# Low parts of the output-projection weights on GpSimd, and attention tiles of layer 0 opened in another order

## The chip, the core and the metric

The kernel is one program on one core of a Trainium2 chip (trn2). The metric is the device time of one execution in microseconds (us); lower is better. TensorE is called PE here, VectorE DVE, ScalarE ACT, GpSimd POOL, and SyncE's DMA queue SP, as the profile does.

## What is computed

A two-layer diffusion backbone over 512 latent tokens and 256 context tokens of width 1024. Each layer is a mixer and then an MLP, and each of the two ends in a residual sum and a layer norm:

```python
x = layer_norm(ALPHA * x + m_lat[2] * y_lat, ln_g[l, 0], ln_b[l, 0])
x = layer_norm(ALPHA * x + m_lat[5] * mlp(x * (1 + m_lat[4]) + m_lat[3], mlp_w1[l], mlp_w2[l]), ln_g[l, 1], ln_b[l, 1])
```

Here `y_lat` is the mixer's heads times `w_out`, and `mlp(u)` is `square(relu(u @ w1)) @ w2`. In layer 0 the same is done for the context tokens. The mixer of layer 0 runs gated linear attention (GLA) beside banded-window attention (GQA); the mixer of layer 1 runs RWKV-7 beside latent attention. All is in float32.

## The kernel before

Every dense product is made from three passes: each float32 operand is split into a high part (`whi`, `hi`, rounded to the fp32r format by ACT, L323) and a low part (`wlo`, `lo`, the remainder, a subtraction on DVE, L324), and `mm3` (L341 to L348) issues high by high (L344), high by low activation (L346) and low weight by high (L348). `weights` (L326) opens the tiles of one weight block of 128x1024 (`wraw` from the DMA, 5 buffers in layer 0's second half and shared with the `araw` loads; `whi` and `wlo`, 2 buffers each) and calls `split` (L321), whose last argument can name another engine for the low part.

`project` (L1001) makes an output projection in two parts of the tokens: in layer 0 all 512 latent tokens (part 0) and then the 256 context tokens (part 1). In each part it goes over eight weight blocks d = 0 to 7; in layer 0 the blocks are loaded and split again for part 1, in layer 1 they are kept (`keep`, `kept`). After part 0, the layer norm of the latent tokens (`norm`, L1038) is a generator that is advanced twice after each block of part 1. So beside the matmuls of part 1 these run:

- L1054 and L1062: mean and variance on PE, from `sums` and the squares (L1066, ACT); L1074 is the reciprocal root `lnr`.
- L1078: DVE multiplies `z` by `lnr`, eight pieces (here z0 to z7).
- L1092: DVE makes `lnu`, L1091: ACT makes the high part of the next activations, L1094: POOL makes their low part `actlo`, again eight pieces each (lnu0 to lnu7, lo0 to lo7).
- L1020 and L1024: DVE adds each block's product into `z` and `sums`.

Behind the projection come the first two weight blocks of the next dense stage, called m0 and m1 below (L323, L324 again). Layer 0 has two such projections: the mixer's (the **first site**, 475 to 517 us of the trace) and the MLP's last (the **second site**, 1042 to 1084 us).

`mixer0` (L858) starts the attention at about 200 us: it closes the weight pool, opens the pool `mb` in its space, and opens there some constants (`zerob`, `identb`, `maskb`, L973 to L981), then the level tiles of GLA (`gla_setup`, L486, with memsets of POOL, L494 and L496), then in `gqa` (L712) the tiles `mE`, `sel` (three small ACT operations, L728), `q2` and `gp`. A tile `mt`, from which `maskb` is cast, takes one of the four `Dt` buffers that GLA's decays also use (L597).

The order in which each engine runs its instructions is made at build time by a scheduler from priorities and dependencies. Every engine runs its own list strictly in order.

## Time and profile before

| what | value |
|---|---|
| median of 3 runs | 2068.6 us (2066.54 to 2073.67) |
| profiled execution | 2074.32 us |
| its span, first to last instruction | 2072.4 us |
| PE busy | 1942.7 us, 94% |
| DVE busy | 1315.2 us, 63% |
| ACT busy | 962.1 us, 46% |
| POOL busy | 297.2 us, 14% |
| mean granted clock of PE | 0.968 |

Busy shares are averages over the whole program. A row of the timeline gives the start of an instruction (or of several alike), how long it took, its engine, line and tiles, and in brackets how long its engine stood idle before it and what it waited for.

### The profile page before, as it was taken

How to read it: one execution, taken by the hardware profiler on the slowest of the kernel's cores; microseconds unless marked ns; L12 is line 12 of the kernel's file. 1: busy time of each engine (PE TensorE's matmuls, PEld its weight loads, DVE VectorE, ACT ScalarE, POOL GpSimd, SP SyncE). 2: the span in 40 equal slices, each digit the busy share in tenths (PEclk: the TensorE clock that was granted, in tenths of full speed). 3: DMA queues.
4: the chain of work that ended last, by engine and by line, in shares of the span. 5: the costliest groups of instructions: out<-in, count | busy, mean ns of one | idle time of the engine just before them, and what ended most of it. 6: DMA issues, size and time to landing. Idle time of an engine off the chain costs nothing.

```text
span 2072.4 us, 35378 instructions
## 1 busy us (share of the span) xinstructions
PE 1942.7 (94%) x14256; PEld 1617.3 (78%) x14256; DVE 1315.2 (63%) x2394; ACT 962.1 (46%) x1852; POOL 297.2 (14%) x503
## 2 busy tenths in 40 slices
PE   7998799999999999999989999988889889999998
PEld 6887666677788888888877877757776788888887
DVE  8785999638897566534484554467876655544454
ACT  5526777535522222222255655766664544333332
POOL 0002666302100000000021020023231020000001
PEclk9999799999999999999999998998999999999999
DMA  8650000063454455313243100000000503332241
GB/s 297 203 171 14 1 2 1 1 211 104 140 169 138 143 158 152 112 51 97 82 147 120 46 9 13 13 9 2 3 7 29 173 28 96 110 94 86 92 137 41
DMA packets 67048, 181.67 MB, mean 88 GB/s; under 512 B 7491, under 2 KB 12355, under 8 KB 66757
## 3 DMA queue, kind: packets, MB, share of 16 engines
q1 hardware_dynamic: 66884, 179.42, 27.8%
q8 instruction: 112, 1.84, 0.4%
q14 instruction: 52, 0.42, 0.1%
HBM read 172.83 MB, written 5.51 MB: 86 GB/s over the span
## 4 chain that ended last, share of the span: by engine, by line
PE 71%; DVE 15%; ACT 7%; issue 3%; DMA 2%; POOL 1%; SPq 0%; DVEq 0%; ACTq 0%; POOLq 0%
PE mm L346 18%; PE mm L348 18%; PE mm L344 17%; DMA araw<-in_ada_r_dram 2%; PE var L1062 2%; PE ms L1454 2%; PE mo L1480 1%; PE gab L1612 1%; DVE wlo L324 1%; DVE aprod L392 1%; DVE z L1078 1%; PE go L789 1%; DMA wraw<-in_w_m_dram 1%; PE gx L1728 1%; PE st L1494 1%
## 5 line engine op out<-in xcount | busy, mean ns | idle before, releaser
L323 ACT CAST whi<-wraw 128x1024 fp32r<-128x1024 f32 (+2 forms) x253 | 221.5, 879 | 639.7 <-PE mm L346 559.9
L344 PE MATMUL mm<-acthi,whi 128*128 128x512 f32 (+1 forms) x1464 | 444.8, 350 | 15.4 <-ACT whi L323 13.5
L348 PE MATMUL mm<-acthi,wlo 128*128 128x512 f32 (+1 forms) x1464 | 439.1, 346 | 8.7 <-DVE wlo L324 8.5
L346 PE MATMUL mm<-actlo,whi 128*128 128x512 f32 (+1 forms) x1464 | 443.8, 349 | 2.4 <-POOL actlo L1094 2.2
L324 DVE TENSOR_TENSOR wlo<-wraw,whi 128x1024 fp32r<-128x1024 f32 (+2 forms) x253 | 256.5, 1017 | 219.0 <-ACT whi L323 214.6
L344 PEld LDWEIGHTS mm<-acthi,whi 128*128 128x128 f32 x1464 | 251.1, 191 | 55.6 <-ACT whi L323 16.0
L348 PEld LDWEIGHTS mm<-acthi,wlo 128*128 128x128 f32 x1464 | 251.8, 192 | 48.8 <-DVE wlo L324 12.6
L346 PEld LDWEIGHTS mm<-actlo,whi 128*128 128x128 f32 x1464 | 251.2, 191 | 39.0 <-POOL actlo L1094 4.1
L348 PE MATMUL mm<-hh,wlo 128*128 128x512 f32 (+1 forms) x832 | 253.1, 342 | 3.6 <-DVE wlo L324 3.6
L346 PE MATMUL mm<-hl,whi 128*128 128x512 f32 (+1 forms) x832 | 254.7, 344 | 0.1
L344 PE MATMUL mm<-hh,whi 128*128 128x512 f32 (+1 forms) x832 | 254.1, 343 | 0.0
L1094 POOL TENSOR_TENSOR actlo<-lnu,acthi 128x256 fp32r<-128x256 f32 (+1 forms) x48 | 60.8, 1281 | 720.6 <-DVE lnu L1092 632.9
L348 PEld LDWEIGHTS mm<-hh,wlo 128*128 128x128 f32 x832 | 144.3, 189 | 24.3 <-DVE wlo L324 4.2
L346 PEld LDWEIGHTS mm<-hl,whi 128*128 128x128 f32 x832 | 143.6, 189 | 19.3 <-issue 0.7
L344 PEld LDWEIGHTS mm<-hh,whi 128*128 128x128 f32 x832 | 142.8, 189 | 20.0 <-issue 1.0
L1166 DVE SCALAR_TENSOR_TENSOR z<-mm,mod,z 128x512 f32<-128x512 f32 (+1 forms) x144 | 94.1, 659 | 97.4 <-PE mm L348 97.4
L392 DVE SCALAR_TENSOR_TENSOR araw<-araw,scb 128x1024 f32<-128x1024 f32 x80 | 97.8, 1222 | 53.4 <-DMA araw<-in_ada_r_dram 52.5
L1020 DVE SCALAR_TENSOR_TENSOR z<-mm,mod,z 128x256 f32<-128x256 f32 (+1 forms) x64 | 34.9, 548 | 82.0 <-PE mm L348 80.9
L323 ACT CAST hh<-relu 128x512 fp32r<-128x512 f32 (+1 forms) x100 | 50.5, 534 | 76.3 <-DVE relu L1118 76.3
L616 POOL TENSOR_TENSOR lk<-kd,Dt 64x128 f32<-64x128 f32 x144 | 76.2, 529 | 31.9 <-ACT Dt L598 12.3
L392 DVE SCALAR_TENSOR_TENSOR aprod<-araw,scb 128x1024 bf16<-128x1024 f32 x48 | 58.6, 1221 | 26.8 <-DMA araw<-in_ada_r_dram 26.7
L324 DVE TENSOR_TENSOR hl<-relu,hh 128x512 fp32r<-128x512 f32 (+1 forms) x100 | 56.1, 587 | 26.5 <-ACT hh L323 26.1
(461 smaller groups left out, 3241.4 us busy)
## 6 DMA issues: line engine op xcount, KB each, us to landing
araw<-in_ada_r_dram SPq DMA_DIRECT2D x80, 512.0 KB, 3.7
wraw<-in_w_dram SPq DMA_DIRECT2D x72, 512.0 KB, 3.6
wraw<-in_w_dram SPq DMA_DIRECT2D x144, 256.0 KB, 2.7
wraw<-in_w_s_dram SPq DMA_DIRECT2D x31, 512.0 KB, 3.7
wraw<-in_w_o_dram SPq DMA_DIRECT2D x22, 512.0 KB, 3.7
scraw<-in_ada_sc_dram SPq DMA_DIRECT2D x8, 512.0 KB, 5.7
shraw<-in_ada_sh_dram SPq DMA_DIRECT2D x8, 512.0 KB, 6.0
x<-in_xT_dram SPq DMA_DIRECT2D x8, 384.0 KB, 5.7
```

Source lines behind the costliest of these rows:

```text
L323: self.nc.scalar.copy(hi, raw)
L324: (eng or self.nc.vector).tensor_tensor(lo, raw, hi.bitcast(F32), op=ALU.subtract)
L344: mm(o, whi, ahi[:, sl], start=first, stop=False)
L346: mm(o, whi, alo[:, sl], start=False, stop=False)
L348: mm(o, wlo, ahi[:, sl], start=False, stop=last)
L392: self.nc.vector.scalar_tensor_tensor(pr, raw, 1.0, self.scb[:, w], op0=ALU.mult, op1=ALU.mult, accum_out=out(w))
L616: nc.gpsimd.tensor_tensor(K[r, :, x], kk[r, :, x], d[r, :, x], op=ALU.mult)
L1020: nc.vector.scalar_tensor_tensor(zs, o, self.mod[:, l, self.wh(i, parts), g, d:d + 1], zs, op0=ALU.mult, op1=ALU.add)
L1062: nc.tensor.matmul(var, self.c('o1024', 0, P), sq, start=(k == 0), stop=(k == KT - 1))
L1094: eng.tensor_tensor(lo[:, k, sl], u, hi[:, k, sl].bitcast(F32), op=ALU.subtract)
L1166: nc.vector.scalar_tensor_tensor(z[:, d, sl], o, self.mod[:, l, self.wh(i, parts), 5, d:d + 1], z[:, d, sl], op0=ALU.mult, op1=ALU.add)
L1454: mm(s_[:, j], a[:, c], b[:, j * 384:j * 384 + 384], start=st, stop=sp_)
```

## The change

It does three things.

1. `weights` takes an engine for the low part, and `project` gives it POOL for the blocks d = 1, 3, 5 and 7 of every part after the first. In layer 0 that moves 4 of the 8 low parts of part 1 from DVE to POOL at each site, 8 instructions of 128x1024 in all. In layer 1 the blocks of the second half are the kept ones, and nothing moves.
2. In the attention of layer 0, `gla_setup` is called before the constants, so the level tiles and their memsets come first and `zerob`, `identb` and `maskb` after them; one `q2` and one `gp` buffer are opened in the middle of the level tiles (`late`, called at level 8) and handed to `gqa` through `early`.
3. `sel` lives in the outer pool `m0` (`mx_`), whose space was not used by weights.

```diff
--- before.py
+++ after.py
@@ -323,7 +323,7 @@
         self.nc.scalar.copy(hi, raw)
         (eng or self.nc.vector).tensor_tensor(lo, raw, hi.bitcast(F32), op=ALU.subtract)
 
-    def weights(self, src, n=1024, keep=None, lead=PW):
+    def weights(self, src, n=1024, keep=None, lead=PW, eng=None):
 
         raw = self.wp.tile([P, 1024], F32, tag="wraw", name="wraw")
         pool, bufs, d = (self.wp, 2, '') if keep is None else (keep[0], 1, keep[1])
@@ -334,7 +334,7 @@
             m = n // len(src)
             for i, s in enumerate(src):
                 self.nc.sync.dma_start(raw[:, i * m:i * m + m], s)
-            self.split(raw[:, :n], hi[:, :n], lo[:, :n])
+            self.split(raw[:, :n], hi[:, :n], lo[:, :n], eng)
         return hi[:, :n], lo[:, :n]
 
     def mm3(self, whi, wlo, ahi, alo, first, last, outs):
@@ -483,7 +483,7 @@
         nc.scalar.activation(tmp, tmp, AF.Ln, bias=self.c('one'))
         nc.scalar.activation(out, tmp, AF.Exp, scale=-1.0)
 
-    def gla_setup(self, m0):
+    def gla_setup(self, m0, mid=lambda: None):
 
         nc = self.nc
         i = len(self.lev)
@@ -494,6 +494,8 @@
             nc.gpsimd.memset(lk[h], 0.0)
             if h >= 16:
                 nc.gpsimd.memset(lq[h], 0.0)
+            if h == 8:
+                mid()
         self.lev.append((lk, lq))
 
     def gla_head(self, m0, mx_, h, qd, kd, vt, a1T, g):
@@ -709,7 +711,7 @@
             for _ in a:
                 yield
 
-    def gqa(self, m0, mx_, queries, KS, K2, vg, hi, lo):
+    def gqa(self, m0, mx_, queries, KS, K2, vg, hi, lo, early):
 
 
 
@@ -723,7 +725,7 @@
             nc.gpsimd.memset(t, 0.0)
             mE.append(t)
         sink = slice(96, 99)
-        sel = m0.tile([99, 192], F32R, name="sel")
+        sel = mx_.tile([99, 192], F32R, name="sel")
         for i in range(3):
             nc.scalar.activation(sel[sink, i * 64:i * 64 + 64], self.c('ident', 0, 64)[sink], AF.Identity,
                                  scale=0.0, bias=self.c('one')[sink] if i != 1 else 0.0)
@@ -732,7 +734,7 @@
 
         def scores(h):
             kv, qs = h // 4, QS[h]
-            q2[h] = Q2 = m0.tile([99, T], F32R, name="q2", bufs=2)
+            q2[h] = Q2 = early.pop('q2') if 'q2' in early else m0.tile([99, T], F32R, name="q2", bufs=2)
 
             nc.gpsimd.memset(Q2[64:67].bitcast(F32), 0.0)
             for t0, n in PARTS:
@@ -800,7 +802,8 @@
                             mm(b[:, (n - n0) * P:(n - n0 + 1) * P], self.identb, self.maskb[0 if n < j else 1],
                                start=False, stop=False)
                 mm(b, K2[kv][:, ks], Q2[0:67, qr], start=False, stop=True)
-                p = m0.tile([P, 512], F32, name="gp", bufs=3)[:, 0:(n1 - n0) * P]
+                p = early.pop('gp') if 'gp' in early else m0.tile([P, 512], F32, name="gp", bufs=3)
+                p = p[:, 0:(n1 - n0) * P]
                 nc.scalar.activation(p, b, AF.Exp)
                 pv()
                 pend.append((ob[:, qr], j, p, j == 4))
@@ -970,6 +973,12 @@
             mhi, mlo = self.act_tiles()
             self.psum(PG[0], u=PG[1], q=PG[2], qo=PG[3])
             with tc.tile_pool(name="mb", bufs=1, reuse_waits="tile") as mb:
+                early = {}
+
+                def late():
+                    early['q2'] = mb.tile([99, T], F32R, name="q2", bufs=2)
+                    early['gp'] = mb.tile([P, 512], F32, name="gp", bufs=3)
+                self.gla_setup(mb, late)
                 self.zerob = mb.tile([P, P], BF16, name="zerob")
                 nc.gpsimd.memset(self.zerob, 0.0)
                 self.identb = mb.tile([P, P], BF16, name="identb")
@@ -979,7 +988,6 @@
                 nc.sync.dma_start(mt, self.a['band'])
                 for i in range(2):
                     nc.gpsimd.tensor_copy(self.maskb[i], mt[:, i * P:(i + 1) * P])
-                self.gla_setup(mb)
 
                 def queries(i):
 
@@ -989,7 +997,7 @@
                             nc.scalar.copy(a[r, sl], qg[i][r, sl])
                             nc.vector.tensor_tensor(a[o, sl], qg[i][r, sl], a[r, sl].bitcast(F32), op=ALU.subtract)
                     return mhi.k(4 + i), mlo.k(4 + i)
-                att = self.gqa(mb, m0, queries, KS, K2, vg, mhi, mlo)
+                att = self.gqa(mb, m0, queries, KS, K2, vg, mhi, mlo, early)
                 for i, _ in enumerate(self.gla(mb, setup, g, qd, kd, og, mhi, mlo)):
                     if i % 5 < 2:
                         next(att, None)
@@ -1009,7 +1017,8 @@
         for i, (t0, m) in enumerate(parts):
             sl = slice(t0, t0 + m)
             for d in range(KT):
-                wh, wl = kept.get(d) or self.weights(ws[d], keep=keep and (keep, d), lead=lead)
+                wh, wl = kept.get(d) or self.weights(ws[d], keep=keep and (keep, d), lead=lead,
+                                                      eng=nc.gpsimd if i and d % 2 else None)
                 if keep:
                     kept[d] = wh, wl
                 o = self.bank("mm")[:, :m]
```

Three places of the instruction order matter. The numbers in the names are those of the tiles.

DVE at the first site, after the second `lnu`, before. `wlo_5042`, `wlo_5079`, `wlo_5116` are the low parts of blocks 5, 6 and 7 of part 1; `mm_4993` is the product of block 4.

```order
L324 TENSOR_TENSOR wlo_5042<-wraw_5040,whi_5041 128x1024
L1092 TENSOR_SCALAR lnu_4978<-z_4504,gb_4824 128x512
L1078 TENSOR_TENSOR z_4504<-z_4504,lnr_4931 128x512
L324 TENSOR_TENSOR wlo_5079<-wraw_5077,whi_5078 128x1024
L1092 TENSOR_SCALAR lnu_4983<-z_4504,gb_4824 128x512
L1020 SCALAR_TENSOR_TENSOR z_4504<-mm_4993,mod_117,z_4504 128x256
L1078 TENSOR_TENSOR z_4504<-z_4504,lnr_4931 128x512
L1024 TENSOR_TENSOR sums_4524<-sums_4524,z_4504 128x256
L1092 TENSOR_SCALAR lnu_5021<-z_4504,gb_4824 128x512
L324 TENSOR_TENSOR wlo_5116<-wraw_5114,whi_5115 128x1024
```

The same stretch of DVE with the change:

```order
L1087 TENSOR_TENSOR z_4504<-z_4504,lnr_4931 128x512 x2
L1101 TENSOR_SCALAR lnu_4978<-z_4504,gb_4824 128x512
L1101 TENSOR_SCALAR lnu_4983<-z_4504,gb_4824 128x512
L1029 SCALAR_TENSOR_TENSOR z_4504<-mm_4993,mod_117,z_4504 128x256
L1087 TENSOR_TENSOR z_4504<-z_4504,lnr_4931 128x512
L324 TENSOR_TENSOR wlo_5079<-wraw_5077,whi_5078 128x1024
L1033 TENSOR_TENSOR sums_4524<-sums_4524,z_4504 128x256
L1101 TENSOR_SCALAR lnu_5021<-z_4504,gb_4824 128x512
L1087 TENSOR_TENSOR z_4504<-z_4504,lnr_4931 128x512 x2
L1101 TENSOR_SCALAR lnu_5026<-z_4504,gb_4824 128x512
```

Blocks 5 and 7 have left this queue, and block 6 (`wlo_5079`) now stands behind one more `z` and one more `lnu`. The low parts of m0 and m1 (`wlo_5157`, `wlo_5163`) stand further down: that of m0 was ahead of the last `z` and the last two `lnu`, and is now behind all of them.

POOL at the first site with the change. Before, the eight `actlo` stood there alone.

```order
L324 TENSOR_TENSOR wlo_4841<-wraw_4839,whi_4840 128x1024
L324 TENSOR_TENSOR wlo_4936<-wraw_4934,whi_4935 128x1024
L1103 TENSOR_TENSOR actlo0_4790<-lnu_4968,acthi0_4788 128x512
L1103 TENSOR_TENSOR actlo0_4790<-lnu_4973,acthi0_4788 128x512
L324 TENSOR_TENSOR wlo_5042<-wraw_5040,whi_5041 128x1024
L1103 TENSOR_TENSOR actlo0_4790<-lnu_4978,acthi0_4788 128x512
L1103 TENSOR_TENSOR actlo0_4790<-lnu_4983,acthi0_4788 128x512
L1103 TENSOR_TENSOR actlo0_4790<-lnu_5021,acthi0_4788 128x512
L324 TENSOR_TENSOR wlo_5116<-wraw_5114,whi_5115 128x1024
L1103 TENSOR_TENSOR actlo0_4790<-lnu_5026,acthi0_4788 128x512
L1103 TENSOR_TENSOR actlo0_4790<-lnu_5031,acthi0_4788 128x512
L1103 TENSOR_TENSOR actlo0_4790<-lnu_5036,acthi0_4788 128x512
```

POOL makes blocks 1 and 3 ahead of the first `actlo`, block 5 behind the second and block 7 behind the fifth. The second site has the same lists with other tile numbers.

DVE at the start of the attention, before:

```order
L990 TENSOR_TENSOR actlo0_1897<-qg0_82,actlo0_1897 64x512
L597 TENSOR_TENSOR Dt_2041<-ld_1576 128x256
L618 TENSOR_TENSOR lq64_1_1917<-qd0_91,Dt_1952 64x2x64 x2
L618 TENSOR_TENSOR lq32_1_1921<-qd0_91,Dt_1997 64x4x32 x2
L964 SCALAR_TENSOR_TENSOR og_90<-mm_1777,col_65,og_90 128x512
L964 SCALAR_TENSOR_TENSOR og_90<-mm_1778,col_65,og_90 128x256
L597 TENSOR_TENSOR Dt_2060<-ld_1576 128x256
L990 TENSOR_TENSOR acthi0_1895<-qg0_82,acthi0_1895 64x512
L990 TENSOR_TENSOR acthi1_1896<-qg0_82,acthi1_1896 64x256
L990 TENSOR_TENSOR actlo1_1898<-qg0_82,actlo1_1898 64x256
L990 TENSOR_TENSOR acthi0_1895<-qg1_83,acthi0_1895 64x512
```

and with the change:

```order
L998 TENSOR_TENSOR actlo0_1897<-qg0_82,actlo0_1897 64x512
L620 TENSOR_TENSOR lq64_1_1907<-qd0_91,Dt_1954 64x2x64 x2
L620 TENSOR_TENSOR lq32_1_1911<-qd0_91,Dt_1998 64x4x32 x2
L967 SCALAR_TENSOR_TENSOR og_90<-mm_1777,col_65,og_90 128x512
L967 SCALAR_TENSOR_TENSOR og_90<-mm_1778,col_65,og_90 128x256
L998 TENSOR_TENSOR acthi0_1895<-qg0_82,acthi0_1895 64x512
L998 TENSOR_TENSOR acthi1_1896<-qg0_82,acthi1_1896 64x256
L998 TENSOR_TENSOR actlo1_1898<-qg0_82,actlo1_1898 64x256
L998 TENSOR_TENSOR acthi0_1895<-qg1_83,acthi0_1895 64x512
L998 TENSOR_TENSOR acthi1_1896<-qg1_83,acthi1_1896 64x256
L998 TENSOR_TENSOR actlo0_1897<-qg1_83,actlo0_1897 64x512
```

The decays `Dt_2041` and `Dt_2060` no longer stand ahead of the splits of the queries (L990, now L998); they come after ten of those splits and behind the first row maximum (L749, now L751). The second row maximum stood ahead of GLA's `ld` (L514) and its scans (L524), and now stands behind four of the scans.

## Rows read from the trace of the kernel before

**Rows 1.** Timeline of DVE, first site: start us, us, instruction, idle before.

```profile
473.62 1.22 DVE L324 TENSOR_TENSOR wlo<-wraw,whi 128x1024 fp32r<-128x1024 f32 x1
...
490.02 1.29 DVE L1078 TENSOR_TENSOR z<-z,lnr 128x512 f32<-128x512 f32 x2 [2.63 <-ACT lnr L1074]
491.23 0.54 DVE L1092 TENSOR_SCALAR lnu<-z,gb 128x512 f32<-128x512 f32 x1
491.69 0.48 DVE L1020 SCALAR_TENSOR_TENSOR z<-mm,mod,z 128x256 f32<-128x256 f32 x1
492.08 1.45 DVE L1092 TENSOR_SCALAR lnu<-z,gb 128x512 f32<-128x512 f32 x1
493.46 0.41 DVE L1024 TENSOR_TENSOR sums<-sums,z 128x256 f32<-128x256 f32 x1
493.79 1.76 DVE L1078 TENSOR_TENSOR z<-z,lnr 128x512 f32<-128x512 f32 x1
495.48 1.21 DVE L324 TENSOR_TENSOR wlo<-wraw,whi 128x1024 fp32r<-128x1024 f32 x1
...
497.67 2.30 DVE L324 TENSOR_TENSOR wlo<-wraw,whi 128x1024 fp32r<-128x1024 f32 x1
```

**Rows 2.** Timeline of POOL, first site.

```profile
491.95 1.31 POOL L1094 TENSOR_TENSOR actlo<-lnu,acthi 128x512 fp32r<-128x512 f32 x1 [73.69 <-DVE lnu L1092]
493.68 1.33 POOL L1094 TENSOR_TENSOR actlo<-lnu,acthi 128x512 fp32r<-128x512 f32 x1 [0.42 <-DVE lnu L1092]
497.29 1.59 POOL L1094 TENSOR_TENSOR actlo<-lnu,acthi 128x512 fp32r<-128x512 f32 x1 [2.29 <-DVE lnu L1092]
```

**Rows 3.** Timeline of PE, first site: first use of block 1, then the waits.

```profile
475.99 0.28 PE L348 MATMUL mm<-acthi,wlo 128*128 128x256 f32 x1
...
496.75 0.58 PE L348 MATMUL mm<-acthi,wlo 128*128 128x256 f32 x1 [2.16 <-DVE wlo L324]
...
504.40 0.39 PE L348 MATMUL mm<-acthi,wlo 128*128 128x256 f32 x1 [0.21 <-DVE wlo L324]
...
508.30 0.50 PE L348 MATMUL mm<-acthi,wlo 128*128 128x512 f32 x1 [0.53 <-DVE wlo L324]
...
512.91 0.50 PE L348 MATMUL mm<-acthi,wlo 128*128 128x512 f32 x1 [1.55 <-DVE wlo L324]
...
516.93 0.70 PE L1054 MATMUL mu<-sums,col 128*128 128x256 f32 x2 [0.56 <-DVE sums L1024]
```

**Rows 4.** Timeline of PE, second site: waits from m0 on.

```profile
1075.84 0.50 PE L348 MATMUL mm<-acthi,wlo 128*128 128x512 f32 x1 [0.53 <-DVE wlo L324]
...
1081.58 0.50 PE L346 MATMUL mm<-actlo,whi 128*128 128x512 f32 x1 [0.92 <-POOL actlo L1094]
...
1083.44 0.98 PE L1054 MATMUL mu<-sums,col 128*128 128x256 f32 x2 [1.12 <-DVE sums L1024]
```

**Rows 5.** Timeline of POOL: two-input operations of other widths, from elsewhere.

```profile
187.40 1.84 POOL L544 TENSOR_TENSOR qt<-qt,qd 128x768 f32<-128x768 f32 x1 [2.52 <-ACT qt L540]
...
538.49 0.78 POOL L1094 TENSOR_TENSOR actlo<-lnu,acthi 128x256 fp32r<-128x256 f32 x1 [0.75 <-DVE lnu L1092]
```

**Rows 6.** Busy time by window: PE, PEld, DVE, ACT, POOL, then granted PE clock.

```profile
496.70:500.00 3.30, 3.25 (x15) 3.26 (x16) 3.30 (x4) 2.77 (x4) 1.59 (x1) 0.50 0.53 159
```

**Rows 7.** Timeline at the start of the attention: PE, DVE, ACT, POOL.

```profile
206.18 2.93 PE L508 MATMUL z<-a1T,con 48*128 48x512 f32 x4 [3.52 <-DVE og L964]
...
227.54 0.80 PE L645 MATMUL o<-A,vt 128*128 128x128 f32 x2 [8.31 <-DVE A L663]
...
208.44 0.42 DVE L597 TENSOR_TENSOR Dt<-ld 128x256 f32<-128x256 f32 x1 [1.93 <-POOL lk L616]
...
205.38 0.72 ACT L728 ACTIVATE sel<-col 3x64 fp32r<-3x64 f32 x3
...
205.06 1.07 POOL L494 MEMSET lk<- 128x256 f32 x4
```

**Rows 8.** Busy time by window inside the attention, same columns as rows 6.

```profile
260.00:300.00 40.00, 37.10 (x261) 26.37 (x260) 38.86 (x105) 30.82 (x90) 25.59 (x46) 1.00 0.00 1
```

## The prediction

> **What bounds the kernel now.** I read the page's busy shares first: PE is busy for 94% of the span, so a gain can only come out of PE's waits. I then read PE's timeline at the three places that the change touches, and the timelines of DVE, POOL and ACT beside each wait. At the first site PE does not wait until block 5, whose low weights come late: 2.16 us. Then it waits 0.21, 0.53, 1.55 and 0.56 us, 5.0 us in all [rows 3]. The second site repeats this 567.5 us later; from m0 on its waits are 0.53, 0.92 and 1.12 us [rows 4]. DVE has no idle time there from 490 us on, row follows row [rows 1]: it is what PE waits for.
>
> What holds DVE up is POOL. Alone, a `z` piece takes 0.65 us (two in 1.29), but the one issued at 493.79 us takes 1.76 [rows 1]. POOL's `actlo` had begun at 493.68 and ended at 495.01 [rows 2]; the `z` ended 0.54 us after that. The low part of block 6, issued at 497.67, takes 2.30 us and ends 1.09 us after POOL's end at 498.88; the `lnu` issued at 492.08 takes 1.45 us and ends 0.27 us after POOL's end at 493.26 [rows 1, 2]. In turn POOL's third operation takes 1.59 us where the first took 1.31, since it was issued while DVE ran a `z`. So these operations of DVE and POOL take turns: whichever runs keeps the other out until its end. `z<-mm,mod,z` (L1020), with one input from PSUM, is not held: it took its 0.48 us with POOL's start inside it [rows 1, 2].
>
> **The price of a low part on POOL.** No row of before shows a POOL operation of two inputs at 128x1024. The other widths take 0.78 us (256), 1.31 (512) and 1.84 (768) [rows 2, 5], 0.53 per 256 columns, which gives 2.37 us. The bounds are twice the 512, 2.62, and DVE's own 1.21 [rows 1]; I take 2.37, next to the 768 row. So each moved block frees 1.14 us of DVE (1.09 plus the overlap of its ends) and takes 2.37 us of the turns that DVE needs. The Trainium skill, GPSIMD Engine Reference, section 3.1, gives 4497 ns for 2048 columns, an estimate of 2.25 us here; by it each site would come out some 0.25 us shorter.
>
> **Site by site.** Blocks 1 and 3 cost nothing. Block 1's low part was made from 473.62 to 474.84 and first used at 475.99 [rows 1, 3]: on POOL it takes 1.15 us longer, which is just that slack. If the cover fails it costs up to a microsecond per site. Block 3 has matmuls of a whole block more in front of it, and DVE has no hurry there.
>
> From 493.79 us I write the new lists down with the turn rule. A waiting operation goes when the other engine's ends; held ones end 0.54 (`z`), 0.28 (`lnu`) or 1.09 us (low part) after it, and `sums` take 0.34. z2 ends at 495.55 as before; POOL makes block 5 from 495.5 to 497.9, where DVE had it at 496.7, and PE's wait of 2.16 becomes 3.4. Then z3 498.4, lnu2 and lnu3 499.3, lo2 500.6, z4 501.1, lo3 502.4, block 6 503.5 (before 499.97 [rows 1]), `sums` and lnu4 504.3, z5 504.8, lo4 506.1, z6 506.6, block 7 on POOL 509.0 (before, PE went on with it at 504.40 [rows 3]), lnu5 and lnu6 509.7, lo5 511.0, z7 511.5, lo6 512.8, lnu7 and `sums` 513.4, lo7 514.7, and only then m0's low part, 515.6. Before, PE went on with m0 at 508.30 [rows 3]. PE itself would be there in time: the rest of a block takes 3.4 us (504.40 to 508.30 less the wait of 0.53 [rows 3]), so blocks 5 to 7 end near 508. So PE starts m0 7.3 us late. What follows takes some of it back: the wait of 1.55 for m1 goes (two L1020, one `sums` and 1.14 us of DVE bring it to 517.8, beside ten matmuls of 0.24 us, a twentieth of the 4.8 us from 1075.84 to the wait that ends at 1081.58 [rows 4]), and so does the 0.56 for `sums`. **First site: 7.3 - 2.1 = +5.2 us.** At the second site the waits of 0.92 and 1.12 go, as m0 starts when lo7 is done: **+5.3 us**. Bounds: +0.4, if only the extra turn time counts (two blocks by 1.23, less the 2.1 of later waits), and +7.3, if nothing is taken back.
>
> What queues behind the moved steps: POOL's `actlo` and SP's weight loads. A `wraw` buffer is now given back up to 4.7 us later (block 7), and the loads and `araw` behind it on SP wait that long; they serve blocks used after m1, over 10 us on, so I cost this at nothing. If that cover failed it would cost those 4.7 us once per site.
>
> **The attention.** DVE's 1.93 us of idle before a decay, which waited for a `Dt` buffer that POOL was still reading [rows 7], go: that decay now stands ten splits later. `sel` leaves 0.72 us of ACT ahead of the queries' splits [rows 7], so these are ready when DVE comes. The ten memsets now run ahead of `zerob`, which makes it 2.5 us later (0.25 each [rows 7]); PE waits for `og` until 206.18 anyway, so that costs nothing, and up to 2.5 us if it did not. The row maximum of L749 moves from ahead of GLA's scans to behind some, which changes their order, not their sum. PE's wait of 8.31 us for DVE, which ends at 227.54 [rows 7], then ends 1.9 us sooner, and since DVE is busy 38.86 of 40 us further on [rows 8] the shift stays. Bounds: -2.65 (both idle and `sel`) and +2.5. I take **-1.9 us**.
>
> **The sum.** 5.2 + 5.3 - 1.9 = +8.6 us. The profiled execution took 2074.3 us (span 2072.4), 5.7 above the median of the runs, so this is 2082.9 on its scale and **2077.2 us** as a median, +0.42%. PE's clock could add to it: after the wait of 2.16 us it was granted 0.50, the 1.2 GHz level, from 496.7 to 500 us [rows 6]. Now the last wait before m0 lies on the path; such a spell behind it costs half of 3.3, about 1.65 us per site. I leave it for the upper end.
>
> **Rivals.**
> (a) *POOL does the wide operations beside DVE.* DVE then loses two low parts of 1.14 us at each site ahead of m0, and PE's waits shrink by 2.3 us per site: -4.6 - 1.9 = -6.5, 2062.1 us. It decides where z3 ends: before block 5's low part is done, and this case holds. Against it stand all the held rows above. The Trainium skill, Perfetto Trace Analysis, section Optimizing Scalar/DVE Operations, says that offloading a saturated DVE to GPSIMD may make sense, and adds that the shared read port may spoil it; the trace bears out the second half. Chance 0.10.
> (b) *Only the extra turn time counts*, the lower bound at both sites: +0.8 to +2, less 1.9: about 2068.6. For it: PE already waits at many places, and a wait that ends late hides others. Against it: m0's low part stands behind every `lnu` now. Chance 0.22.
> (c) *The attention gives nothing*, since ACT's casts set the pace of the splits instead of DVE: +10.5, 2079.1 us. ACT is as full as DVE in that stretch. Chance 0.14.
> (d) *The clock falls at both sites*, or block 1 comes late: +12, 2080.6 us. Chance 0.06.
> The forecast has 0.48. That the change would not do what it says is excluded by the instruction order; in layer 1 nothing moves.
>
> **How the numbers follow.** Within 0.3% is within 6.2 us, about what a measurement of this kernel can tell from no change. Slower by more: some three quarters of the forecast (0.35), nearly all of (c) and (d) (0.19): 0.54. Faster by more: half of (a) and a little of (b): 0.09. The rest, 0.37, within. The forecast's own range is 2072 to 2082 (the clock above, half absorbed waits below); to hold 8 in 10 over all cases it goes from 2065 to 2084.
>
> **What would show it.** In the changed profile POOL's `wlo` rows should take about 2.4 us, and the DVE row under each should end 0.5 to 1.1 us after it. PE's wait for block 5 should be over 3 us, with new waits above 1 us for blocks 6, 7 and m0, while those for m1, `actlo` and `sums` are gone. PE's 8.31 us wait should end near 225.6. The forecast is wrong if DVE rows run through POOL's `wlo`, or if PE starts m0 less than 3 us later than before, measured from block 5's first matmul.

## The result and the profile after

| | before | after |
|---|---|---|
| median of 9 runs each, same chips | 2073.61 us (2066.54 to 2075.82) | 2083.32 us (2073.48 to 2089.49) |
| profiled execution | 2074.32 us | 2087.1 us |
| its span | 2072.4 us | 2085.3 us |

The ratio of after to before is **1.0051, 95% interval 1.0033 to 1.0069**: 10.6 us slower (6.8 to 14.3); the two medians differ by 9.7. The forecast was a ratio of 1.0042 (2077.2 over 2068.6), inside that interval. Its time was missed: 2083.3 us lies above the forecast's own range, 2072 to 2082, though inside the wider one over all cases, 2065 to 2084. It is 6.1 us above the forecast's 2077.2, and 5.0 of these are the median of before, which is 2073.6 over nine runs where three had given 2068.6.

Busy time of the engines, on the page of after:

```profile
PE 1948.8 (93%) x14256; PEld 1622.0 (78%) x14256; DVE 1315.3 (63%) x2386; ACT 962.5 (46%) x1852; POOL 313.8 (15%) x511
```

DVE has lost eight instructions of 1.2 us and is as busy as before (1315.2 us): what it gave away came back as time in which it is held. The first site shows how. DVE's timeline there, columns as in [rows 1]:

```profile
496.39 4.53 DVE L1087 TENSOR_TENSOR z<-z,lnr 128x512 f32<-128x512 f32 x2
500.85 1.00 DVE L1101 TENSOR_SCALAR lnu<-z,gb 128x512 f32<-128x512 f32 x2
...
503.46 2.28 DVE L324 TENSOR_TENSOR wlo<-wraw,whi 128x1024 fp32r<-128x1024 f32 x1
...
508.75 3.06 DVE L1101 TENSOR_SCALAR lnu<-z,gb 128x512 f32<-128x512 f32 x2
...
515.20 2.29 DVE L324 TENSOR_TENSOR wlo<-wraw,whi 128x1024 fp32r<-128x1024 f32 x1
...
518.53 1.21 DVE L324 TENSOR_TENSOR wlo<-wraw,whi 128x1024 fp32r<-128x1024 f32 x1
```

POOL's timeline, the four low parts it now makes:

```profile
475.76 2.79 POOL L324 TENSOR_TENSOR wlo<-wraw,whi 128x1024 fp32r<-128x1024 f32 x1 [69.15 <-ACT whi L323]
482.62 2.55 POOL L324 TENSOR_TENSOR wlo<-wraw,whi 128x1024 fp32r<-128x1024 f32 x1 [4.08 <-ACT whi L323]
...
497.58 2.79 POOL L324 TENSOR_TENSOR wlo<-wraw,whi 128x1024 fp32r<-128x1024 f32 x1
...
508.24 2.83 POOL L324 TENSOR_TENSOR wlo<-wraw,whi 128x1024 fp32r<-128x1024 f32 x1
```

Two `z`, 1.29 us when nothing stands beside them [rows 1], take 4.53: the second waits for POOL's low part of block 5, which ends at 500.37, and ends 0.55 us later. Two `lnu` beside block 7 take 3.06 instead of 1.00 (the row at 500.85). So the low part of block 6 is made from 503.46 and that of m0 only from 515.20, behind every `lnu`. On PE:

```profile
500.42 0.39 PE L348 MATMUL mm<-acthi,wlo 128*128 128x256 f32 x1 [3.21 <-POOL wlo L324]
505.80 0.58 PE L348 MATMUL mm<-acthi,wlo 128*128 128x256 f32 x1 [2.23 <-DVE wlo L324]
511.12 0.38 PE L348 MATMUL mm<-acthi,wlo 128*128 128x256 f32 x1 [0.77 <-POOL wlo L324]
...
517.54 0.50 PE L348 MATMUL mm<-acthi,wlo 128*128 128x512 f32 x1 [3.05 <-DVE wlo L324]
...
520.87 0.59 PE L1063 MATMUL mu<-sums,col 128*128 128x256 f32 x2
```

These answer to [rows 3]: the waits for block 5, block 7 and m0 have gone from 2.16, 0.21 and 0.53 us to 3.21, 0.77 and 3.05; block 6, which PE did not wait for, now costs 2.23; and the waits for m1 and `sums` (1.55 and 0.56) are gone. The second site has waits on blocks 5 and 7 and on m0 as well, and none on block 6, where PE ran at a granted clock of 0.53 and 0.62 (1072 to 1080 us) and came late itself (PE again, after):

```profile
1072.87 0.58 PE L348 MATMUL mm<-hh,wlo 128*128 128x256 f32 x1 [3.22 <-POOL wlo L324]
1083.57 0.39 PE L348 MATMUL mm<-hh,wlo 128*128 128x256 f32 x1 [1.84 <-POOL wlo L324]
1089.99 0.80 PE L348 MATMUL mm<-acthi,wlo 128*128 128x512 f32 x1 [3.05 <-DVE wlo L324]
```

**Where the 12.9 us of span went.** I took the same matmul in both traces and subtracted its starts:

| place | before | after | shift | what lies between |
|---|---|---|---|---|
| last GLA matmuls ahead of `zerob` | 200.23 | 202.51 | +2.28 | start-up, where nothing was moved |
| end of the 8.31 us wait | 227.54 | 227.50 | -0.04 | attention: -2.32 |
| decay matmuls | 239.88 | 240.88 | +1.00 | +1.04 at 237 to 239 |
| GQA, last head | 410.15 | 411.39 | +1.24 | +0.24 |
| the same, 5 us on | 415.47 | 418.38 | +2.91 | +1.67 at 413 to 417 |
| before the first site's `z` | 489.87 | 492.49 | +2.62 | -0.29 |
| m0 at the first site | 508.30 | 517.54 | +9.24 | **6.6 us late** |
| a wait behind the site | 538.78 | 545.30 | +6.52 | first site in all: **+3.9** |
| variance, second site | 1053.82 | 1061.36 | +7.54 | +1.0 |
| m0 at the second site | 1075.84 | 1089.99 | +14.15 | **6.6 us late** |
| layer 1's first stages | 1114.24 | 1128.00 | +13.76 | second site in all: **+6.2** |
| end of the span | 2072.4 | 2085.3 | +12.9 | -0.9 |

The first line is not the change: the kernels below, whichever part of the change they have, stand there from -4.2 to +2.7 us against before. The attention's gain is PE's, at the place of [rows 7]:

```profile
207.17 0.29 PE L657 MATMUL base<-zerob 128*128 128x128 bf16 x1 [4.13 <-POOL zerob L983]
...
227.50 0.80 PE L647 MATMUL o<-A,vt 128*128 128x128 f32 x2 [2.85 <-DVE A L665]
```

`zerob` comes late, but PE then waits another 0.64 us for `og`, which came last in the kernel before too; and the 8.31 us wait is 2.85 now, the rest of it split among two earlier ones of 1.78 and 2.88 us. The two losses of the attention are the same work at a lower clock. PE's eight `lev` matmuls, before and then after:

```profile
237.07 1.13 PE L661 MATMUL lev<-lq,lk 128*128 128x128 f32 x8
```

```profile
237.04 1.92 PE L663 MATMUL lev<-lq,lk 128*128 128x128 f32 x8
```

and the windows around both places; columns: window, length, PE, PEld, DVE, ACT and POOL busy, granted clock of PE, DMA share, GB/s. Before, and then after:

```profile
238.00:240.00 2.00, 2.00 (x26) 1.70 (x26) 1.88 (x10) 0.95 (x5) 1.42 (x4) 1.00 0.01 4
...
414.00:416.00 2.00, 2.00 (x13) 1.36 (x11) 0.00 (x0) 0.95 (x3) 0.00 (x0) 1.00 0.00 0
```

```profile
238.00:240.00 2.00, 2.00 (x14) 2.00 (x14) 1.20 (x7) 0.90 (x4) 1.41 (x4) 0.66 0.02 4
...
414.00:416.00 2.00, 2.00 (x6) 0.83 (x5) 0.00 (x0) 0.00 (x0) 0.00 (x0) 0.50 0.00 0
```

At 414 us PE was granted 0.50, its 1.2 GHz level, and the same matmuls (those from 410.15 to 415.47 us in before) took 1.67 us longer. It had waited 0.63 and 0.53 us just ahead, and these two waits stand in before as well, without a fall.

### The profile page after: what moved, and what is told of

Read it like the earlier page. It is cut to its first block, busy times and chain, and to the rows that moved or that the text cites. A ratio compares the mean times of both kernels' runs of the same rounds, so it can differ in the third digit from the quotient of the medians.

```text
span 2085.3 us, 35375 instructions
## 1 busy us (share of the span) xinstructions
PE 1948.8 (93%) x14256; PEld 1622.0 (78%) x14256; DVE 1315.3 (63%) x2386; ACT 962.5 (46%) x1852; POOL 313.8 (15%) x511
## 3 DMA queue, kind: packets, MB, share of 16 engines
q8 instruction: 112, 1.84, 0.4%
## 4 chain that ended last, share of the span: by engine, by line
PE 69%; DVE 14%; ACT 7%; issue 4%; DMA 4%; POOL 1%; SPq 0%; DVEq 0%; ACTq 0%; POOLq 0%
PE mm L348 17%; PE mm L346 17%; PE mm L344 17%; DMA araw<-in_ada_r_dram 3%; PE var L1071 2%; PE ms L1463 1%; DVE wlo L324 1%; PE mo L1489 1%; PE gab L1621 1%; DVE aprod L392 1%; PE gx L1737 1%; DVE araw L392 1%; DVE z L1087 1%; PE go L791 1%; PE st L1503 1%
## 5 line engine op out<-in xcount | busy, mean ns | idle before, releaser
L324 DVE TENSOR_TENSOR wlo<-wraw,whi 128x1024 fp32r<-128x1024 f32 (+2 forms) x245 | 250.1, 1024 | 222.2 <-ACT whi L323 218.0
L344 PEld LDWEIGHTS mm<-hh,whi 128*128 128x128 f32 x832 | 144.8, 190 | 20.7 <-issue 1.0
L324 POOL TENSOR_TENSOR wlo<-wraw,whi 128x1024 fp32r<-128x1024 f32 x8 | 21.9, 2738 | 572.6 <-ACT whi L323 572.6
L1103 POOL TENSOR_TENSOR actlo<-lnu,acthi 128x256 fp32r<-128x256 f32 (+1 forms) x48 | 56.6, 1199 | 149.2 <-ACT acthi L1100 75.1
```

Of the source, the lines that this page charges most:

```text
L324: (eng or self.nc.vector).tensor_tensor(lo, raw, hi.bitcast(F32), op=ALU.subtract)
L344: mm(o, whi, ahi[:, sl], start=first, stop=False)
L1103: eng.tensor_tensor(lo[:, k, sl], u, hi[:, k, sl].bitcast(F32), op=ALU.subtract)
```

## The experiments

All ratios are to before, run on the same chip; 1% is 20.7 us.

| kernel | what it is | ratio (95%) | us |
|---|---|---|---|
| e2_proj | POOL low parts alone | 1.0046 (1.0025 to 1.0068) | +9.5 |
| e3_b13 | of these, blocks 1 and 3 | 0.9999 (0.9981 to 1.0018) | -0.2 |
| e4_b57 | of these, blocks 5 and 7 | 1.0051 (1.0031 to 1.0072) | +10.6 |
| e13_b7 | of these, block 7 | 1.0021 (1.0006 to 1.0035) | +4.4 |
| e5_sub | extra subtractions on POOL | 1.0035 (1.0019 to 1.0051) | +7.3 |
| e6_copy | extra copies on POOL | 1.0026 (1.0007 to 1.0045) | +5.4 |
| e6_set | extra memsets on POOL | 1.0012 (0.9991 to 1.0032) | +2.5 |
| e8_actdve | `actlo` of layer 0 on DVE | 0.9909 (0.9890 to 0.9928) | -18.9 |
| e12_all | `actlo` of both layers on DVE | 0.9908 (0.9888 to 0.9929) | -19.1 |
| e11_swap | e8, and POOL low parts as in the change | 0.9972 (0.9960 to 0.9985) | -5.8 |
| e9_lk | `lk` of the attention on DVE | 1.0145 (1.0121 to 1.0170) | +30 |
| e1_att | attention edit alone | 1.0011 (0.9990 to 1.0032) | +2.3 |
| e1_again | the same kernel again | 0.9977 (0.9958 to 0.9995) | -4.8 |
| e14_sel | `sel` in the outer pool alone | 0.9996 (0.9980 to 1.0012) | -0.8 |
| e10_both | e8 and the attention edit | 0.9914 (0.9897 to 0.9931) | -17.8 |
| e15_allatt | e12 and the attention edit | 0.9886 (0.9858 to 0.9914) | -23.6 |

**The parts of the change, one by one.** The projections without the attention, and then two blocks of them at a time:

```diff
+  eng=nc.gpsimd if i and d % 2 else None        # e2_proj
+  eng=nc.gpsimd if i and d in (1, 3) else None  # e3_b13
+  eng=nc.gpsimd if i and d in (5, 7) else None  # e4_b57
+  eng=nc.gpsimd if i and d == 7 else None       # e13_b7
```

> The projection half alone: POOL makes the low parts of blocks 1, 3, 5 and 7 of part 1; the attention is as before. Theory (POOL and DVE take turns and m0's low part stands behind all of them): +4.4 us at the first site and +4.4 to +6.2 at the second, in all +9 to +11 us; m0's wait near 3 us at both sites, 6.6 us late. Rival (only the extra turn time counts): +1 to +3 us. Rival (the attention edit is the cause): within 2 us of before.

> Only blocks 1 and 3 of part 1 on POOL, attention as before. Theory: in that stretch DVE has idle time and block 1 has just enough slack, so nothing, within 1.5 us of before. Rival (any POOL low part costs its share of the turns): about half of the whole, +5 us. Rival (the slack of block 1 is not there): +1 to +2 us.

> Only blocks 5 and 7 of part 1 on POOL, attention as before. Theory: the whole price of the projections is here, +9 to +11 us, the same as with all four blocks. Rival (any POOL low part costs its share): +5 us.

> Before, with only block 7 of part 1 on POOL. Theory (each of blocks 5 and 7 costs its own turns and pushes m0's low part): block 7 alone gives a part of the 10.6 us of both, +3 to +6 us, and m0 is 2 to 4 us late at each site. Rival (all of it comes from block 5, whose wait opens the stretch; block 7 is hidden): within 1.5 us of before. Rival (all of it comes from block 7, behind which the rest of the list stands): +9 us or more.

The whole price is that of the projections (1.0046, against 1.0051 for the change), and of these, of blocks 5 and 7; blocks 1 and 3 cost nothing. A share of the price per POOL instruction is excluded: it depends on whether DVE is late there. Block 7 alone has some 0.4 of the price of both, and in its trace m0 starts 2.1 us late at each site. In e2_proj m0 starts 6.6 us late at both sites again (514.54 against 508.30 with an entry of -0.37 us, 1082.22 against 1075.84 with -0.21). I expected a wait near 3 us ahead of it at both: it is 3.05 at the first and 1.55 at the second, where PE came later itself, at a granted clock of 0.57 from 1076 to 1080 us. In all its first site costs 3.9 us, as the change's does, and its second 3.4 (+3.19 at 1114.24 us, the place of the table, against -0.21), where the change's cost 6.2. The difference is the clock behind m0. Before, the change, and e2_proj (windows, columns as above):

```profile
1084.00:1088.00 4.00, 4.00 (x12) 3.15 (x12) 3.55 (x8) 1.58 (x4) 0.00 (x0) 0.61 0.50 173
...
1092.00:1096.00 4.00, 4.00 (x19) 3.13 (x18) 1.94 (x3) 2.87 (x6) 0.00 (x0) 1.00 0.00 0
```

```profile
1092.00:1096.00 4.00, 4.00 (x11) 3.13 (x10) 0.52 (x2) 0.00 (x0) 0.00 (x0) 0.50 0.86 257
```

```profile
1084.00:1088.00 4.00, 4.00 (x19) 3.34 (x18) 0.76 (x2) 0.69 (x2) 0.00 (x0) 1.00 0.92 248
```

Before had its own fall at 1084 us (4 us at 0.61, so 1.6 us lost), the change a longer one behind m0, e2_proj none. Added to e2_proj's 3.4, the 1.6 us give 5.0 for the second site without the clock. So the same instructions cost 2.8 us more in one profile than in the other; the medians are the price.

Such spells also stand where the change does not reach. In layer 1, from 1241 to 1256 us of before, PE's mean granted clock is 0.55 in before and 0.62 over the same matmuls in the change; in seven other traces whose edits do not reach layer 1 either, e2_proj among them, it is 1.00, and these matmuls take 5.3 us less than in before. Before, and then e2_proj:

```profile
1248.00:1252.00 4.00, 4.00 (x14) 3.90 (x14) 1.04 (x2) 1.31 (x2) 0.00 (x0) 0.50 0.00 0
```

```profile
1248.00:1252.00 4.00, 3.43 (x18) 2.93 (x19) 1.99 (x3) 2.25 (x4) 0.00 (x0) 1.00 0.00 0
```

That is half of the change's whole price, so the spans of two single profiles say little about it; the shifts within one stretch and the medians do.

**Turns or lateness?** If POOL's low part were only late, an operation on POOL that nobody waits for would cost nothing. So DVE keeps all low parts, and POOL gets an extra operation on `wraw` behind blocks 5 and 7, whose result is not read:

```diff
+            if more:   # i and d in (5, 7), layer 0
+                self.nc.gpsimd.tensor_tensor(raw, raw, hi.bitcast(F32), op=ALU.subtract)  # e5_sub
+                self.nc.gpsimd.tensor_copy(raw, hi.bitcast(F32))                          # e6_copy
+                self.nc.gpsimd.memset(raw, 0.0)                                           # e6_set
```

> Before, with every low part still made by DVE, and two more subtractions on POOL per site: after DVE has made the low part of block 5 (and of block 7), POOL subtracts the high part from `wraw` once more, in place, 128x1024, and nobody reads the result. So no low part comes later through POOL's own slowness; only the turns are taken. Theory (turns): each of POOL's 2.55 us is missing to DVE, 5.1 us per site, less some 2 us that later waits give back: +6 to +10 us, and the DVE rows beside end 0.3 to 1.1 us after POOL's. Rival (it is only the lateness of a low part made on a slower engine): within 1.5 us of before, DVE rows as short as before.

> The same, but the two extra operations of POOL per site are copies of the high part over `wraw` (128x1024, one input, not two). Theory in the form that the prediction gave it (operations of two inputs take turns): DVE's rows beside are not held, time within 1.5 us of before. Rival (any operation of POOL that reads and writes SBUF takes a turn): DVE rows end after POOL's copies, and the time goes up by the copies' own length, some +4 to +10 us.

> The extra-operation test with a memset of `wraw` (128x1024) on POOL in place of the copy: it reads nothing. Theory (only operations that read SBUF take a turn): DVE's rows beside are as short as before, time within 1.5 us of before. Rival (any operation of POOL on SBUF takes a turn): the `z` beside ends after the memset, as it did after the copy, and the time rises by 3 to 6 us.

e5_sub, DVE, POOL and PE's wait ahead of m0:

```profile
497.35 2.87 DVE L1081 TENSOR_TENSOR z<-z,lnr 128x512 f32<-128x512 f32 x1
...
497.05 2.61 POOL L339 TENSOR_TENSOR wraw<-wraw,whi 128x1024 f32<-128x1024 f32 x1 [1.76 <-DVE wlo L324]
...
512.97 0.50 PE L350 MATMUL mm<-acthi,wlo 128*128 128x512 f32 x1 [2.73 <-DVE wlo L324]
```

e6_copy, DVE and POOL:

```profile
497.68 1.52 DVE L1081 TENSOR_TENSOR z<-z,lnr 128x512 f32<-128x512 f32 x1
...
497.37 1.29 POOL L339 COPY wraw<-whi 128x1024 f32<-128x1024 f32 x1 [1.75 <-DVE wlo L324]
```

e6_set, DVE and POOL:

```profile
494.53 1.37 DVE L1095 TENSOR_SCALAR lnu<-z,gb 128x512 f32<-128x512 f32 x1
...
503.02 2.38 DVE L1081 TENSOR_TENSOR z<-z,lnr 128x512 f32<-128x512 f32 x2
...
494.66 0.96 POOL L339 MEMSET wraw<- 128x1024 f32 x1 [1.75 <-DVE wlo L324]
...
504.20 0.95 POOL L339 MEMSET wraw<- 128x1024 f32 x1
```

The `z` ends at 500.22, 0.56 us behind POOL's subtraction (499.66), and at 499.20, 0.54 us behind POOL's copy (498.66). Lateness is excluded as the only cause: nobody reads the result of the extra work, and it costs 7.3 and 5.4 us. Nor does it act through POOL's later `actlo`: in e5_sub the waits of PE that grew are for low parts that DVE makes, m0 starts 4.4 us late at each site, and the one wait for `actlo`, at the second site, is 0.90 us as before (0.92). My "two inputs" for POOL's side fell as well: a copy has one and takes a turn as long as itself. The memset holds `lnu` (1.37 instead of 0.54, ending 0.28 us behind it), but not `z`: the two `z` at 503.02 take 2.38, as the two in before at 504.27 did. In both kernels the first of the two is held by an `actlo`; the second runs beside the memset in e6_set, and beside nothing of POOL's in before, and takes no longer. My theory for e6_set had both `z` and `lnu` free. Its time is not told from before.

**The exchange the other way.** If a turn of POOL costs DVE more than the work itself, POOL's `actlo` should go to DVE:

```diff
-                eng = nc.gpsimd
+                eng = nc.gpsimd if l else nc.vector   # e8_actdve
+                eng = nc.vector                       # e12_all
```

> Before, with `actlo` (layer 0, latent and context tokens) made by DVE instead of POOL: the change run the other way. Theory (turns): DVE makes 128x512 in 0.65 us where POOL takes a turn of 1.31, so DVE gains about 0.65 us per piece, 5.2 us per site over eight pieces; PE's waits at the first site (5.0 us) shrink to 1 to 3: 4 to 8 us faster than before in all, and a little more from the context pieces. Rival (DVE and POOL work beside each other): DVE gets 8 times 0.65 us more work at each site, 2 to 10 us slower.

> `actlo` on DVE in layer 1 as well (16 more pieces of 128x256). Theory (turns): DVE's 0.41 us in place of POOL's 0.78, so up to 6 us of turns come free; PE waits little there, so 0 to 3 us faster than with layer 0 alone: 0.9895 to 0.991. Rival (DVE's list is what layer 1 waits for): 1 to 4 us slower than that.

> `actlo` of layer 0 on DVE and in exchange the low parts of blocks 1, 3, 5 and 7 of part 1 on POOL, so that POOL has nothing else at the sites. Theory (turns): blocks 5 and 7 take 2.55 us of turns each where DVE takes 1.14, 2.8 us per site, and PE, which hardly waits any more, feels it: 3 to 7 us slower than `actlo` on DVE alone, so 0.992 to 0.994 of before. Rival (POOL's op cost only because `actlo` stood in POOL's queue behind and before it): 2 to 5 us faster than `actlo` on DVE alone, below 0.990.

e8_actdve, the engines, a stretch of DVE at the first site, and PE's one wait up to m0:

```profile
PE 1933.6 (94%) x14256; PEld 1610.2 (78%) x14256; DVE 1308.9 (64%) x2426; ACT 961.8 (47%) x1852; POOL 251.6 (12%) x471
```

```profile
497.35 0.69 DVE L1094 TENSOR_TENSOR actlo<-lnu,acthi 128x512 fp32r<-128x512 f32 x1
497.95 0.69 DVE L1078 TENSOR_TENSOR z<-z,lnr 128x512 f32<-128x512 f32 x1
498.55 1.22 DVE L324 TENSOR_TENSOR wlo<-wraw,whi 128x1024 fp32r<-128x1024 f32 x1
...
497.49 0.39 PE L348 MATMUL mm<-acthi,wlo 128*128 128x256 f32 x1 [0.17 <-DVE wlo L324]
```

DVE has 32 instructions more, 16 of 0.69 us and 16 of 0.41 (128x256), 17.6 us, and is busy 6.3 us **less**: 23.9 us in which POOL had held it are gone. No row of the stretch is held, and PE waits 0.17 us where it waited 5.0. The 18.9 us are over twice the 4 to 8 that I expected. In the trace the first site gives 7.5 us (from 489.87 to 600 us of before) and the second 9.7, of which before's own fall at 1084 us is 1.6. I had expected 2 to 4 at each: but nearly all of the waits go, and so does the spell at 0.50 behind the wait of 2.16 [rows 6], in which PE lost some 1.65 us; e8_actdve is granted 1.00 from 496.7 to 500 us. Of the first site's 7.5 us, 6.3 are gained up to m1. This is the version that beats both kernels. With `actlo` of layer 1 on DVE too it is the same within the intervals.

e11_swap puts the change's POOL low parts on top, with nothing else in POOL's list at the sites. I expected 3 to 7 us for them; it is 0.9972 against 0.9909, some 13 us. Its POOL, DVE and PE:

```profile
494.03 3.68 POOL L324 TENSOR_TENSOR wlo<-wraw,whi 128x1024 fp32r<-128x1024 f32 x1 [10.73 <-ACT whi L323]
...
495.42 2.57 DVE L1093 TENSOR_SCALAR lnu<-z,gb 128x512 f32<-128x512 f32 x1
...
497.76 0.58 PE L348 MATMUL mm<-acthi,wlo 128*128 128x256 f32 x1 [2.44 <-POOL wlo L324]
```

So the price does not come from POOL's own queue. A low part on POOL waits for its turn too: 3.68 us instead of 2.55. Against e8_actdve this trace loses 4.0 us at the first site and 6.3 at the second, with granted clocks of 0.66 (496 to 500 us) and 0.84 and 0.73 (1068 to 1076) behind the waits; the other 3 us of the 13 I did not place.

**The limit of that.** The same exchange inside the attention:

```diff
-                nc.gpsimd.tensor_tensor(K[r, :, x], kk[r, :, x], d[r, :, x], op=ALU.mult)
+                nc.vector.tensor_tensor(K[r, :, x], kk[r, :, x], d[r, :, x], op=ALU.mult)
```

> Before, with the level products `lk` of the attention (144 of 64x128, 0.53 us each on POOL, 76 us in all) made by DVE. Theory (turns): DVE is busy 97% of that stretch, but part of this is being held by POOL; DVE's own similar `lq` takes 0.33 us, so 144 times 0.2 us, up to 29 us of turns, come free: 5 to 25 us faster. Rival (they work beside each other): DVE gets 47 us more, up to 40 us slower.

A miss: 30 us slower. The groups of DVE from 200 to 420 us (columns: busy us, mean ns, idle before), before and e9_lk:

```profile
L618 DVE TENSOR_TENSOR lq<-qd,Dt 64x128 f32<-64x128 f32 x66 | 23.8, 361 | 1.2 <-ACT Dt L595 0.3
```

```profile
L616 DVE TENSOR_TENSOR lk<-kd,Dt 64x128 f32<-64x128 f32 x132 | 38.5, 292 | 2.3 <-ACT Dt L595 0.7
...
L618 DVE TENSOR_TENSOR lq<-qd,Dt 64x128 f32<-64x128 f32 x66 | 19.3, 292 | 0.8 <-ACT Dt L595 0.4
```

DVE's like operations were held by 0.07 us each there (361 against 292 ns), 4.6 us over 66 of them, and 38.5 us came on top. Over all its rows of that stretch DVE got back some 15 us. I had taken all of POOL's 76 us for turns; the mean of a row beside tells how much of them collides, and here it is little.

**The attention.** Its edit alone, twice, then only its one line on `sel`, then on top of `actlo` on DVE:

```diff
-        sel = m0.tile([99, 192], F32R, name="sel")
+        sel = mx_.tile([99, 192], F32R, name="sel")   # all of e14_sel
```

> The attention half of the change alone; all low parts are made on DVE as before. Theory (the changed kernel's trace read against the one of before): the wait for the `Dt` buffer and `sel` really go, so that the work at 227 us stands about 2.2 us earlier than at 200 us, relative to before; what was lost later (1.05 us at 238 us and 1.7 us at 413 us) was the same work at a granted clock of 0.50 and comes and goes from run to run. Then this kernel is 0 to 3 us faster than before, about -2, and the lead of 2.2 us at 227 us stands in its trace again. Rival (attention gives nothing): no lead at 227 us, time within 1 us. Rival (the later memsets and constants cost): +1 us or more.

> The attention half alone, a second time. Theory (the lead is real and the clock takes it back): lead of 2.2 us at 227 us, a fall of the granted clock between 408 and 418 us, lead below 0.8 us at 440 us; time within 0.15% of before. Rival (the falls near 412 us were chance, as in 3 of 10 traces without the edit): no fall here, the lead is still over 1 us at 440 us, time 1 to 2 us below before.

> Before, with `sel` alone moved to the outer pool: its three operations leave ACT's list ahead of the queries' splits, and the scheduler then also sets the `Dt` decays behind these splits on DVE. Theory (this order is what gives the lead): a lead of 1.5 to 2.2 us at 227 us without the earlier level tiles; time within 0.15% of before. Rival (the lead needs the earlier level tiles): no lead at 227 us.

> `actlo` of layer 0 on DVE together with the attention half of the change; all low parts of weights on DVE. If the attention's 2.2 us stayed: 2 us faster than `actlo` on DVE alone (0.9909 of before), so 0.990. Theory (the clock takes them back, as in both profiles with this edit): the same as that kernel, 0.991, and a fall of the granted clock near 412 us in its trace.

> `actlo` on DVE in both layers together with the attention half. Theory (clock takes the lead back): the same as `actlo` on DVE in both layers alone, 0.9908, and a fall of the clock between 408 and 418 us. Rival: 0.990 or below, no fall.

Each matmul's start against before, at three places:

| kernel | 200.34 us | 227.54 us | 439.84 us | gain to 228 | left at 440 |
|---|---|---|---|---|---|
| the change | +2.28 | -0.04 | +2.57 | 2.32 | -0.29 |
| e1_att | -0.03 | -2.29 | +0.03 | 2.26 | -0.06 |
| e1_again | -2.10 | -4.33 | -4.38 | 2.23 | 2.28 |
| e10_both | -0.55 | -2.88 | -0.29 | 2.33 | -0.26 |
| e15_allatt | +0.54 | -1.69 | +0.64 | 2.23 | -0.10 |
| e14_sel | +0.17 | -1.91 | -1.76 | 2.08 | 1.93 |

The traces of the other kernels, e9_lk aside, change by at most 0.26 us between the first two places. So the gain is real there, and the line on `sel` with the order that the scheduler then picks is enough for it. My theory that the clock takes it back each time fell: a fall of the granted clock near 412 us stands in four of the five traces with the whole edit, and where it does nothing is left; e1_again has none, and all is left. Of the twelve other traces (before among them, e9_lk left out) three have such a fall and lose 2.0 to 3.0 us between 228 and 440 us. Windows of e1_att and of e1_again:

```profile
412.00:414.00 2.00, 2.00 (x6) 1.13 (x5) 0.00 (x0) 0.12 (x1) 0.00 (x0) 0.50 0.00 0
```

```profile
412.00:414.00 2.00, 2.00 (x11) 1.62 (x10) 0.00 (x0) 0.97 (x2) 0.00 (x0) 1.00 0.00 0
```

e1_again's set of runs was faster (0.9977), but its profile shows one of twelve runs and can't say how often the others fell. e1_att was expected some 2 us faster and came out at +2.3. e10_both came out as the theory said (0.9914, with a fall). e15_allatt has a fall too, but a time of 0.9886 (0.9858 to 0.9914), which fits theory and rival alike. The two sets of one kernel give +2.3 and -4.8 us, a mean of -1.2: both the forecast's -1.9 and zero fit. Whether the edit makes a fall of the clock likelier stays open.

## Why the prediction was wrong: the scale, and a gain that the clock took back

The direction was right, and so was the mechanism at the two sites. Two terms of the sum failed, and a third, the clock, was put at nothing.

- **The scale, the step that took the time out of its range.** I took 5.7 us off the sum on the profiled execution's scale (2082.9) to come to a median of 2077.2, because before's profiled execution stood 5.7 us above the median of three runs. Over nine runs before stands at 2073.6, and the term is 0.7 us. Its 5.0 us are most of the 6.1 us of the miss. Three runs from 2066.5 to 2073.7 us could not fix that base: in the four sets of the experiments (20 to 35 runs each, on three chips) before's median is 2069.6 to 2072.4, and single runs go from 2061.8 to 2082.2. So it was in part luck on which side of 2082 the time fell; the ratio, which needs no base, was inside the interval.
- **The attention, -1.9, "the shift stays".** The first half was right: -2.3 at 227 us, with `zerob` late and still hidden behind `og`. That the shift stays failed in this trace: two falls of the clock took 2.7 us back, and from 200 to 490 us the attention gave +0.3 in all instead of -1.9. Over all runs it is not told from zero. Rival (c), in which the attention gives nothing, had the sum +10.5, and 10.6 was measured; by its reason, ACT setting the pace of the splits, it is excluded, and its ground, that ACT is as full as DVE, does not stand in [rows 8] (30.82 against 38.86 of 40 us).
- **The clock, at nothing.** I left it to the upper end, and it decides 2.8 us at the second site, 2.7 in the attention, and 5.3 in layer 1 where nothing moved, in the trace of before too. Whether a spell costs anything depends on what follows: in before the spell behind the first site's wait of 2.16 us filled a wait. The second site of before has the same wait and no spell (1.00 from 1064 to 1068 us), and PE waits 1.24 us for block 7 there instead of 0.21 and starts m0 no sooner, 567.5 us after the first.
- **Second site, +5.3**: 6.2 in the change's trace and 3.4 in e2_proj's, for the same instructions; corrected for the fall in before, e2_proj's is 5.0, near the term.
- **m0 7.3 us late, 2.1 taken back, +5.2**: 6.6 late at both sites in the change and in e2_proj, and 2.7 taken back at the first, so +3.9. Rival (b), only the extra turn time (+0.4), is excluded by the 6.6 us.
- **The two sites, +10.5**: +9.5 measured (5.2 to 14.1, e2_proj), with the clock in it. In e2_proj's one trace they are 7.3. That the whole came within 2 us of the forecast's +8.6 is in part luck: the first site fell short by 1.3 us, and the attention's 1.9 did not come.
- **Turns of DVE and POOL** (the ground of the forecast): right. The rows of after, e5_sub and e8_actdve show it, and rival (a), POOL beside DVE, is excluded by all three.
- **2.37 us for a low part on POOL**: 2.55 measured without a neighbour, inside the bounds and nearer to the upper one, 2.62, than to the price I took. By the figure of the Trainium skill, GPSIMD Engine Reference, section 3.1, it was an estimate of 2.25: the trace does not agree.
- **Blocks 1 and 3 at nothing**: right (0.9999). Block 1's part ended at 478.55, and PE has no wait for it.
- **Waits**: over 3 us for block 5 (3.21), over 1 for m0 (3.05), those for m1, `actlo` and `sums` gone: right. For block 6 it is 2.23 at the first site and nothing at the second, for block 7 0.77 and 1.84, where I wrote over 1 for both.

## What to carry to other kernels

Before work is moved from DVE to POOL, read the rows of DVE that stand beside POOL's: where they are held, such a piece can cost DVE the whole of POOL's time (2.55 us against 1.14 for a low part, 1.31 against 0.69 for an `actlo`), and the exchange in the other direction is the gain, here 18.9 us. How much it brings is the held time that the rows beside show, not POOL's busy time: where they were held by 0.07 us each, it cost 30 us. A price on a wait also has to say what PE's clock does behind it, since the same instructions at the second site cost 2.8 us more in one trace than in another. And a forecast in microseconds needs a base of more than three runs where single runs differ by 20 us.

## What was not expected of the hardware

- A POOL copy of 128x1024 takes 1.29 us, half of the subtraction's 2.55 and about as long as DVE's subtraction (1.21), and still holds a DVE operation of two SBUF inputs to its end.
- A POOL memset (0.96 us) holds DVE's `lnu`, an operation with scalars and one SBUF input, but not `z`, which has two. The Trainium skill, SBUF — State Buffer, section Who interferes with whom, states just that: two SBUF inputs contend with a POOL instruction that reads SBUF, not with one that only writes, while `tensor_scalar` can enter a mode that contends with POOL. The rows of e6_set agree (1.37 us for `lnu`, 2.38 for two `z` as before); that `lnu` ran in that mode no run here shows.
- The granted clock falls to 0.50 in busy stretches of one trace and not in another of the same kernel (412 us in e1_att, not in e1_again). A spell of some 13 us in layer 1, where the change moves nothing, stands in the trace of before and not in seven others with the same layer 1, and is worth 5.3 us.
